# Two more PSUM banks between the native runs of medium expert pairs, and down weights loaded with two rows side by side

## The chip, the core and the metric

The kernel runs on one core of a Trainium2 chip. The metric is the device time of one execution in microseconds (us), the median of the runs. A second measure is the span of one execution under the hardware profiler, from its first to its last instruction.

The engines are TensorE (PE, with its weight loads as PEld), VectorE (DVE), ScalarE (ACT), GpSimd (POOL) and SyncE (SP, which issues nearly all DMA transfers). SBUF is the memory that the engines read, PSUM the one that TensorE writes, in eight banks of 128 partitions x 512 fp32 columns.

## What is computed

One layer of a decoder for 512 tokens of 1024 fp32 values: an attention part, a mixture of 32 experts of which each token takes four, a gated term and a last norm. The change touches only the experts:

```python
def moe(x, w_router, b_router, w_up, b_up, w_down, b_down):
    ...
    xs = xf[tok]
    h = lax.ragged_dot(xs, w_up, sizes) + b_up[sorted_e]
    g, lin = jnp.split(h, 2, axis=-1)
    g = jnp.minimum(g, SWIGLU_LIMIT)
    lin = jnp.clip(lin, -SWIGLU_LIMIT, SWIGLU_LIMIT)
    act = g * jax.nn.sigmoid(SWIGLU_ALPHA * g) * (lin + 1.0)
    y = lax.ragged_dot(act, w_down, sizes) + b_down[sorted_e]
    y = y * w.reshape(-1)[order][:, None].astype(y.dtype)
    return jax.ops.segment_sum(y, tok, num_segments=n).reshape(B, T, D)
```

Here `xf` is the normed residual, `tok` the token of each row sorted by expert, and `w` the softmax weight of each choice. Per expert `w_up` is 1024 x 2048 and `w_down` 1024 x 1024, all fp32.

## The kernel before

After attention and routing the 32 experts are sorted by how many tokens they got and given kinds: five pairs of a big (B, up to 128 tokens) and a small one (S, up to 64), then eleven pairs of a medium (M, up to 96) and a small one. Expert i is handled by `up(i)`, an activation (`act_big`, `act_medium`, `act_small`) and `down(i)`. M and S experts multiply the fp32 weights as they were loaded (a native run): the tokens stand as stationary tiles of 32 columns, and four matmuls into the four 32-row parts of a PSUM bank go side by side (`halves`). A B expert splits its weights in two rounded parts first.

**Order of a medium pair.** TensorE runs up_medium(i), down(i-1) of the small expert before, up_small(i+1), then **stretch 1**, down(i) of the medium expert, then **stretch 2**, and the next up_medium. `hooks` put other work into the two stretches, and `fence` keeps the order. Stretch 1 has these steps, each with a PSUM bank from `new_x()`:

- two times four transposes of the medium expert's activations (`rest` in `act_medium`, L1353), copied out by ACT (L1355);
- `pair_slots` of the next pair (L1043, L1046): eight small matmuls find which token stands in which slot. Eight copies on DVE bring the result to `v4` and `vx` (L1051, L1055), `fetch` turns it into indices (L993, L995), and POOL gathers the rows of the tokens with two indirect DMAs (L997);
- five times `add` (L1427): three matmuls bring the result of earlier experts back to token order, and DVE adds it to the residual `x` (L1452).

Stretch 2 has the small expert's four transposes (L1333, copied by ACT, L1334), then in turn four times four transposes of the gathered rows (`rows_T`, L1005, copied by ACT, L1011 and L1013) and the last three adds. The bias matmuls of the next run follow (L1261, L1263).

**PSUM.** Pool pU has the banks u0 to u3, pY y0 and y1, and px two banks that `new_x()` hands out in turn; a step whose bank is still read by DVE or ACT waits. up_medium writes u0, u1 and u2, up_small of such a pair u3 and u0, down(i) y0 and y1.

**Weights.** `load_next` issues one transfer of 1 MiB on SP's queue as soon as a slot is free: 128 rows of w_up (8 KB a partition), or 256 rows of w_down, of which partition p gets rows p and p + 128 (two pieces of 4 KB). A pair takes 16 transfers of w_up and 8 of w_down.

The lines of the bank and of the load:

```python
    def new_x():
        return px.tile([128, 512], F32, name="px1")
...
            src = w[:, 256 * c:256 * c + 256, :].rearrange("o (k p) f -> p (o k) f", p=128)
            t = t.rearrange("p (k f) -> p k f", k=2)
```

Of the kernel before, what the change touches and what calls it, by code (L numbers as in the profile page):

```python
# [9 lines left out]
F32 = mybir.dt.float32  # L10
# [9 lines left out]
D = 1024  # L20
# [16 lines left out]
KIND = "BS" * NB + "MS" * (16 - NB)  # L37
EO = (2 * NB - 2, 4)
CAP = {"B": 128, "M": 96, "S": 64}
KW = 5  # L40
NEW = 2
G7 = 7.0 / (1.0 + math.exp(-1.702 * 7.0))
# [16 lines left out]
def f32(ap):  # L59
    return ap.bitcast(F32)  # L60
# [3 lines left out]
def hybrid_block_kernel(  # L64
# [5 lines left out]
    nc = tc.nc  # L70
# [7 lines left out]
    identf = cp.tile([128, 128], F32, name="identf")  # L78
# [96 lines left out]
    if True:  # L175
# [27 lines left out]
        for k in range(KT):  # L203
            pt = pT.tile([128, 512], F32, name="pt")
# [22 lines left out]
        o = 0  # L227
# [493 lines left out]
    def load_next(eng=nc.sync):  # L721
        key = order[nload[0]]
        nload[0] += 1
        e, part, c = key
        t = raw_tile(key)
        raws[key] = t
        if part in ("bu", "bd"):

            src = (b_up if part == "bu" else b_down)[0].rearrange("e (b q f) -> e q b f", q=2, f=512)
            n = FF if part == "bu" else 512  # L730
            for q in range(2):
                eng.dma_start(out=t[64 * q:64 * q + NE, 0:n].rearrange("e (b f) -> e b f", f=512), in_=src[:, q])
            return
        if part in "UD" and e not in ids:

            ids[e] = nc.values_load(idi[0:1, e:e + 1], engines=[mybir.EngineType.SP], min_val=0, max_val=NE - 1)
        if part == "U":
            src = w_up[0, ds(ids[e], 1) if e else slice(0, 1), 128 * c:128 * c + 128, :].rearrange("o p f -> p (o f)")
        else:
            w = {"D": lambda: w_down[0, ds(ids[e], 1) if e else slice(0, 1)], "G": lambda: w_ple_gate,  # L740
                 "W": lambda: w_out[:, 512:]}[part]()
            src = w[:, 256 * c:256 * c + 256, :].rearrange("o (k p) f -> p (o k) f", p=128)
            t = t.rearrange("p (k f) -> p k f", k=2)
        loaded.append(eng.dma_start(out=t, in_=src))

# [28 lines left out]
    for _ in range(NRA):  # L774
        load_next()
# [20 lines left out]
    for t, key in ((bup, "bu"), (bds, "bd")):  # L796
        r = raws.pop((0, key, 0))
# [240 lines left out]
    def pair_slots(i):  # L1038

        oh = ohs[i // 2]  # L1040
        pt = new_x()
        for j in range(NT):
            nc.tensor.matmul(pt[:, 0:8], oh[:, j, 0:128], w4p[:, j, i:i + 2].rearrange("p e a -> p (e a)"),  # L1043
                             start=(j == 0), stop=(j == NT - 1))
        for j in range(NT):
            nc.tensor.matmul(pt[:, 8:12], oh[:, j, 32:160], w4p[:, j, i], start=(j == 0), stop=(j == NT - 1))  # L1046
        u, w, x = slice(0, 64), slice(64, 128), slice(96, 128)
        for e, src in ((i, pt[w, 0:4]), (i + 1, pt[u, 4:8])):
            v = v4[e] = fc.tile([C, 4], F32, name="v4", bufs=6)
            for r in (u, w):  # L1050
                nc.vector.tensor_copy(v[r], src)  # L1051

        v = vx[i] = fc.tile([C, 4], F32, name="vx", bufs=3)
        for r in range(0, 128, 32):
            nc.vector.tensor_copy(v[r:r + 32], pt[x, 8:12])  # L1055
        fetch(i)
        fetch(i + 1)
        nc.vector.tensor_tensor(v[:, 3:4], v[:, 0:1], v[:, 1:2], op=ALU.add)
        for e in (i, i + 1):
            nc.vector.tensor_tensor(wtt[:, e:e + 1], v4[e][:, 0:1], v4[e][:, 1:2], op=ALU.add)  # L1060
# [28 lines left out]
    for m in range(4):  # L1089
        mm = first_rows((3,), (m,))  # L1090
        v = pts[m].rearrange("p (k n c) -> p k n c", n=2, c=C)
# [22 lines left out]
    pU = pool(ectx, "pU", 1, space=PSUM)  # L1114
    pY = pool(ectx, "pY", 1, space=PSUM)
    px = pool(ectx, "px", 2, space=PSUM)
# [4 lines left out]
    def new_y():  # L1121
        return [pY.tile([128, 512], F32, name=f"y{s}") for s in range(2)]

    def new_x():
        return px.tile([128, 512], F32, name="px1")

    def sort_ids():
        pt = new_x()
# [49 lines left out]
    def note():  # L1178
        stretch.append(next(x for x in reversed(nc.cur_bb.bb.instructions) if x.engine == mybir.EngineType.PE))

    @contextmanager
    def fence():

        with ExitStack() as after:
            for x in stretch:
                after.enter_context(tc.issue_after(x))
            stretch.clear()
            yield

    def hooks(between, at, ins):  # L1190
        note()
        for k, f in between:
            if k == at:
                with tc.issue_after(ins):
                    f()
                note()
# [99 lines left out]

    aT = {}

    def swiglu(g, ln, pg, pl):
        nc.scalar.activation(g, pg, AF.Gelu_apprx_sigmoid)  # L1300
        nc.vector.tensor_scalar(ln, pl, 8.0, -6.0, op0=ALU.min, op1=ALU.max)  # L1301
        nc.vector.scalar_tensor_tensor(ln, g, G7, ln, op0=ALU.min, op1=ALU.mult)

    def act_big(i, ps):

        t = aT[i] = ex1.tile([128, 2, KT, C], F32R, name="ab")

        def half(b):
            ln = ex1.tile([C, 512], F32, name="aln", bufs=2)
            swiglu(ex1.tile([C, 512], F32, name="ag"), ln, ps[b], ps[2 + b])  # L1310

            def rest():
                pt = new_x()
                for k in range(4):
                    nc.tensor.transpose(pt[:, k * 128:(k + 1) * 128], ln[:, k * 128:(k + 1) * 128], identf)
                v = pt.rearrange("p (k c) -> p k c", c=C)
                nc.scalar.copy(t[:, 0, 4 * b:4 * b + 4], v)
                nc.vector.tensor_sub(t[:, 1, 4 * b:4 * b + 4], v, f32(t[:, 0, 4 * b:4 * b + 4]))

            return rest  # L1320

        return [half(b) for b in range(2)]

    def act_small(i, ps):

        t = aT[i] = ex2.tile([128, KT, 64], F32, name="am")
        ln = ex1.tile([128, 512], F32, name="aln", bufs=2)
        swiglu(ex1.tile([128, 512], F32, name="ag"), ln, *ps)

        def rest():  # L1330
            pt = new_x()
            for k in range(4):
                nc.tensor.transpose(pt[:, k * 128:(k + 1) * 128], ln[:, k * 128:(k + 1) * 128], identf)  # L1333
            nc.scalar.copy(t.rearrange("p (h k) c -> p h k c", h=2), pt.rearrange("p (k h c) -> p h k c", h=2, c=64))  # L1334

        return [rest]

    def act_medium(i, ps):

        t = ex1.tile([128, 2, KT, C], F32, name="ab").rearrange("p a k c -> p (a k c)")  # L1340
        t = aT[i] = t[:, 0:KT * 96].rearrange("p (k c) -> p k c", c=96)
        tv = t.rearrange("p (h k) c -> p h k c", h=2)
        ln, lx = (ex1.tile([128, 512], F32, name="aln", bufs=2) for _ in range(2))
        swiglu(ex1.tile([128, 512], F32, name="ag"), ln, ps[0], ps[1])
        g, u = ex1.tile([128, 512], F32, name="ag"), slice(64, 128)
        nc.scalar.activation(g[u], ps[2][0:64], AF.Gelu_apprx_sigmoid)
        nc.vector.tensor_scalar(lx, ps[2], 8.0, -6.0, op0=ALU.min, op1=ALU.max)
        nc.vector.scalar_tensor_tensor(lx[u], g[u], G7, lx[u], op0=ALU.min, op1=ALU.mult)

        def rest(src, a, b):  # L1350
            pt = new_x()
            for k in range(4):
                nc.tensor.transpose(pt[:, k * 128:(k + 1) * 128], src[:, k * 128:(k + 1) * 128], identf)  # L1353
            v = pt.rearrange("p (k q) -> p k q", q=128)[:, :, 64 * (a > 0):]
            nc.scalar.copy(tv[:, :, :, a:b], v.rearrange("p k (h c) -> p h k c", h=2))  # L1355

        return [lambda: rest(ln, 0, 64), lambda: rest(lx, 64, 96)]
# [211 lines left out]
    for i in range(NE):  # L1569
# [42 lines left out]
        nexts = gathers(i // 2 + 1) if i + 1 < NE else []  # L1612
        if KIND[i - 1] == "B":
            between = [(-1, f) for f in ahead_of] + [(HA, rest[0])] + list(zip(KS, adds)) + list(zip(HG, nexts))
            with fence():
                note()
                hooks(between, -1, stretch[-1])
                down(i - 1, between, chunks)
        else:
            behind = [f for pair in zip(nexts, adds[KW:] + [None]) for f in pair if f]  # L1620
            between = [(7 if nexts else 3, rest[0])] + [(7, f) for f in (behind or adds[KW:])]
            with fence():
                note()
                hooks([(-1, f) for f in ahead_of + adds[:KW]], -1, stretch[-1])
            with fence():
                down(i - 1, between)
        if i == 2 * NB - 1:

            slots += [[hiA[0], f"{name}{n}", -1] for name in ("hi", "lo") for n in (1, 2)]
            slots += [[mixp, "m8", -1] for _ in range(2)]  # L1630
# [152 lines left out]
```

## Time and profile before

| What | Value |
|---|---|
| runs of the kernel | 1575.9, 1576.07, 1583.03 us; median 1576.07 us |
| the profiled execution | 1576.53 us, its span 1574.9 us |
| PE (matmul) | 1484.1 us busy, 94% of the span |
| PEld (weight loads, beside PE) | 828.3 us, 53% |
| DVE | 717.1 us, 46% |
| ACT | 518.6 us, 33% |
| POOL | 313.0 us, 20% |
| mean granted TensorE clock | 0.979 of full speed |
| DMA | 452.90 MB, mean 288 GB/s; 111648 packets on SP's queue, 71.8% of 16 engines' span |

Times of rows are from the span's start. "Idle before" is how long the engine stood before an instruction, with what ended it. A busy PE is not PE at its peak: the ends of its pipelined matmuls are modelled, so two rows can overlap, and steps between starts say more. The granted clock 1.00 is 2.4 GHz, 0.50 is 1.2 GHz. The DMA share is of all 16 DMA engines and can read a little over 1.

### The profile page before, as it was taken

To read this page: it belongs to the slowest core of one execution; us is meant where nothing else is said; L and a number is where in the kernel's file an instruction comes from. 1 tells how busy PE (TensorE), PEld (TensorE's weight loads), DVE (VectorE), ACT (ScalarE), POOL (GpSimd) and SP (SyncE) were. 2 spreads that over 40 slices of the span, in tenths; PEclk is the share of its full clock that TensorE was granted. 3 is DMA by queue.
4 is the path that set the end of the run, shared out by engine and by line. 5 is a ranking of instruction groups with operands and counts; after the bars stand their busy time and mean duration, and the time that the engine had idled before them with its cause. 6 is when DMAs were issued, how large, how long until landed. Compare 5 with 4: busy or idle time off the path is not lost.

```text
span 1574.9 us, 26212 instructions
## 1 busy us (share of the span) xinstructions
PE 1484.1 (94%) x10421; PEld 828.3 (53%) x10421; DVE 717.1 (46%) x1470; ACT 518.6 (33%) x992; POOL 313.0 (20%) x469
## 2 busy tenths in 40 slices
PE   6999999999889999899899999999999999999997
PEld 5777777788554747565243333434333343433366
DVE  6578788777554856564122122212212221221165
ACT  5556666645443535342011101101110111111154
POOL 5222221122420311303021111203111130301011
PEclk9999999998999999999999999999999999999999
DMA  6240210563599999986999999999999999999611
GB/s 164 59 114 15 75 41 28 171 230 122 214 405 356 383 368 358 400 330 245 417 392 417 396 394 415 390 417 380 416 371 390 378 364 402 357 391 376 243 67 54
DMA packets 116767, 452.90 MB, mean 288 GB/s; under 512 B 11160, under 2 KB 43456, under 8 KB 83872
## 3 DMA queue, kind: packets, MB, share of 16 engines
q1 hardware_dynamic: 111648, 437.51, 71.8%
q0 software_dynamic: 3632, 10.49, 2.3%
q10 hardware_dynamic: 1360, 3.17, 0.5%
q8 instruction: 83, 1.36, 0.4%
q14 instruction: 44, 0.36, 0.1%
HBM read 444.78 MB, written 6.36 MB: 286 GB/s over the span
## 4 chain that ended last, share of the span: by engine, by line
PE 47%; DMA 4%; DVE 3%; ACT 2%; issue 1%; POOL 0%; POOLq 0%; ACTq 0%; DVEq 0%; SPq 0%
PE u L1244 18%; PE y L1244 10%; PE px L1427 5%; PE u L1273 4%; PE y L1390 2%; PE u L1715 2%; DMA raw<-in_w_down_dram 1%; DMA m<-in_w_up_dram 1%; DVE x L1452 1%; PE u L1234 1%; DMA raw<-in_w_up_dram 1%; DMA lo<-in_w_up_dram 1%; PE y L1381 0%; ACT ag L1300 0%; PE px L1333 0%
## 5 line engine op out<-in xcount | busy, mean ns | idle before, releaser
L1301 DVE TENSOR_SCALAR aln<-u 128x512 f32<-128x512 f32 x37 | 25.6, 691 | 380.9 <-PE u L1244 196.1
L1452 DVE TENSOR_TENSOR x<-x,px 128x512 f32<-128x512 f32 x120 | 81.6, 686 | 185.0 <-PE px L1427 184.1
L1300 ACT ACTIVATE ag<-u 128x512 f32<-128x512 f32 x37 | 22.2, 599 | 397.2 <-PE u L1244 176.3
L1244 PE MATMUL u<-raw,xs 128*32 128x512 f32 x976 | 111.2, 596 | 10.4 <-DMA raw<-in_w_up_dram 10.4
L1427 PE MATMUL px<-yb,so 128*128 128x512 f32 x240 | 92.9, 472 | 20.2 <-DVE vx L1055 9.1
L1080 POOL TENSOR_SCALAR so<-tok,v 128x512 fp32r<-128x512 f32 x32 | 52.7, 1648 | 226.1 <-PE px L1427 223.7
L1253 POOL TENSOR_SCALAR bsel<-blk,selp 128x128 fp32r<-128x128 f32 x11 | 6.6, 603 | 432.6 <-PE u L1292 432.6
L1234 PE MATMUL u<-hi,xb 128*128 128x512 f32 x240 | 80.0, 403 | 0.0
L1244 PEld LDWEIGHTS u<-raw,xs 128*32 128x32 f32 x976 | 30.7, 110 | 86.0 <-issue 66.0
L1334 ACT COPY am<-px 128x512 f32<-128x512 f32 x16 | 9.4, 587 | 200.8 <-PE px L1333 200.8
L763 DVE TENSOR_TENSOR lo<-raw,hi 128x1024 fp32r<-128x1024 f32 x50 | 59.3, 1221 | 28.3 <-ACT hi L762 28.3
L1427 PEld LDWEIGHTS px<-yb,so 128*128 128x128 f32 x240 | 43.9, 212 | 48.6 <-DVE x L1452 25.0
L159 PE MATMUL ps<-uh,wlo 128*128 128x512 f32 x160 | 65.3, 408 | 0.0
L762 ACT CAST hi<-raw 128x1024 fp32r<-128x1024 f32 x50 | 50.4, 1048 | 42.9 <-DMA raw<-in_w_down_dram 15.8
L159 PE MATMUL ps<-uh,whi 128*128 128x512 f32 x160 | 64.4, 403 | 0.1
L159 PE MATMUL ps<-ul,whi 128*128 128x512 f32 x160 | 64.2, 401 | 0.0
L1244 PE MATMUL u<-raw,xb 128*32 128x512 f32 x528 | 62.8, 593 | 0.0
L1409 DVE SCALAR_TENSOR_TENSOR ym<-y,wtt,ym 64x512 fp32r<-64x512 f32 x30 | 22.5, 750 | 85.1 <-ACT ym L1408 85.1
L307 ACT ACTIVATE P<-s,nm 128x256 f32<-128x256 f32 (+3 forms) x96 | 50.8, 532 | 21.5 <-DVE nm L306 20.6
L1244 PE MATMUL u<-xn,xs 128*32 128x512 f32 x448 | 52.6, 609 | 5.3 <-ACT hi L762 3.0
L150 POOL TENSOR_TENSOR wlo<-wraw,whi 128x512 fp32r<-128x512 f32 x20 | 31.8, 1594 | 104.8 <-ACT whi L148 79.9
L1427 PE MATMUL px<-ym,so 128*128 128x512 f32 x120 | 52.5, 437 | 0.0
(523 smaller groups left out, 3333.8 us busy)
## 6 DMA issues: line engine op xcount, KB each, us to landing
raw<-in_w_up_dram SPq DMA_DIRECT2D x120, 1024.0 KB, 13.4
raw<-in_w_down_dram SPq DMA_DIRECT2D x61, 1024.0 KB, 11.6
xn<-in_w_up_dram SPq DMA_DIRECT2D x55, 1024.0 KB, 11.7
xn<-in_w_down_dram SPq DMA_DIRECT2D x34, 1024.0 KB, 7.8
hi<-in_w_up_dram SPq DMA_DIRECT2D x28, 1024.0 KB, 14.7
lo<-in_w_up_dram SPq DMA_DIRECT2D x24, 1024.0 KB, 12.0
m<-in_w_up_dram SPq DMA_DIRECT2D x23, 1024.0 KB, 12.4
m<-in_w_down_dram SPq DMA_DIRECT2D x13, 1024.0 KB, 14.6
```

The lines of the kernel that those rows point to most:

```text
L150: nc.gpsimd.tensor_tensor(lo[:, 4:8], raw[:, 4:8], f32(hi[:, 4:8]), op=ALU.subtract)
L159: nc.tensor.matmul(ps, wa[:, k, :], ub[:, k, :], start=(n == 0), stop=(n == 3 * KT - 1))
L307: nc.scalar.activation(P[:, o:o + n], s[:, o:o + n], AF.Exp, bias=nm[:, u:u + 1], accum_out=sm[:, u:u + 1])
L762: split_act.append(nc.scalar.copy(hi[:, w], r[:, w]))
L763: nc.vector.tensor_tensor(lo[:, w], r[:, w], f32(hi[:, w]), op=ALU.subtract)
L1080: nc.gpsimd.tensor_scalar(so[i], tok, v4[i][:, 2:3], None, op0=ALU.is_equal)
L1234: mm = nc.tensor.matmul(ps[s], a, b[:, w], start=(i + k + n == 0), stop=(k == KT - 1 and n == 2))
L1244: mm = nc.tensor.matmul(ps[r:r + 32], x[:, c:c + 32], w, start=start, stop=stop)
L1273: nc.tensor.matmul(ps[2][32 * s:32 * s + 32], x[:, k, 64:96], raw[:, 512 * s:512 * s + 512], start=False, stop=stop)
L1390: mm = nc.tensor.matmul(ps[1][r:r + 32], t[:, 2 * c + m, 64:96], raw[:, o:o + 512], start=(c == 0), stop=(c == 3))
L1427: nc.tensor.matmul(ps, so[o][:, 128 * t:128 * t + 128], y, start=(first and not m), stop=(m == len(terms) - 1))
L1452: nc.vector.tensor_tensor(xs[t][:, w], xs[t][:, w], pt, op=ALU.add)
```

## The change

`new_x()` takes names from a list first: in stretch 1 the eight banks are px, u1, px, u2, px, u1, px, u2, in stretch 2 the first four are u1, px, u2, px and the rest px. The four copies into `v4` go from DVE to ACT. A transfer of w_down gives partition p the neighbouring rows 2p and 2p + 1, one piece of 8 KB, and so the transposes of all activations take every second column (`every`).

```diff
+SP1 = (None, "u1", None, "u2") * 2
+SP2 = ("u1", None, "u2", None)
...
-            src = w[:, 256 * c:256 * c + 256, :].rearrange("o (k p) f -> p (o k) f", p=128)
+
+            src = w[:, 256 * c:256 * c + 256, :].rearrange(
+                "o (p k) f -> p (o k) f" if part == "D" else "o (k p) f -> p (o k) f", p=128)
...
             for r in (u, w):
-                nc.vector.tensor_copy(v[r], src)
+                nc.scalar.copy(v[r], src)
...
+    spare = []
+
     def new_x():
-        return px.tile([128, 512], F32, name="px1")
+        name = spare.pop(0) if spare else None
+        return pU.tile([128, 512], F32, name=name) if name else px.tile([128, 512], F32, name="px1")
...
+    def every(a, k):
+
+        return a[:, 256 * (k // 2):256 * (k // 2) + 256].rearrange("p (c k) -> p k c", k=2)[:, k % 2]
...
-                nc.tensor.transpose(pt[:, k * 128:(k + 1) * 128], src[:, k * 128:(k + 1) * 128], identf)
+                nc.tensor.transpose(pt[:, k * 128:(k + 1) * 128], every(src, k), identf)
...
             with fence():
                 note()
+                spare.extend(SP1)
                 hooks([(-1, f) for f in ahead_of + adds[:KW]], -1, stretch[-1])
+                spare.clear()
             with fence():
+                spare.extend(SP2 if nexts else ())
                 down(i - 1, between)
+                spare.clear()
```

The same line of `transpose` changes in `act_big` and `act_small`. Three places show what moves. The first is PE in stretch 1 of a medium pair, from its transposes (lines stand 4 to 11 further down in the changed kernel; `px1` is a px bank, `u1` and `u2` are banks of pU, the number behind is the use; `aln` holds activations, `w4p` and `sqa` the slots, `yb` and `ym` results of medium and small experts, `so` where they belong). Before:

```order
L1353 MATMUL px1_8132<-identf_60,aln_7960 128x128 [waits DVE_49]
L1353 MATMUL px1_8132<-identf_60,aln_7960 128x128 x3
L1353 MATMUL px1_8138<-identf_60,aln_7961 128x128 [waits DVE_49]
L1353 MATMUL px1_8138<-identf_60,aln_7961 128x128 x3
L1043 MATMUL px1_8144<-w4p_4307,sqa_7970 128x8 [waits Activation_49]
L1043 MATMUL px1_8144<-w4p_4307,sqa_7970 128x8 x3
L1046 MATMUL px1_8144<-w4p_4307,sqa_7970 128x4 x4
L1427 MATMUL px1_8174<-yb_7814,so_7979 128x512 [waits Activation_49]
L1427 MATMUL px1_8174<-yb_7814,so_7981 128x512
L1427 MATMUL px1_8174<-ym_8026,so_7983 128x512 [waits DVE_49]
L1427 MATMUL px1_8179<-yb_7814,so_7979 128x512 [waits DVE_49,PE_49]
L1427 MATMUL px1_8179<-yb_7814,so_7981 128x512
```

Now:

```order
L1364 MATMUL px1_8132<-identf_60,aln_7960 128x128 [waits DVE_49]
L1364 MATMUL px1_8132<-identf_60,aln_7960 128x128 x3
L1364 MATMUL u1_8138<-identf_60,aln_7961 128x128 [waits DVE_49,PE_49]
L1364 MATMUL u1_8138<-identf_60,aln_7961 128x128 x3
L1047 MATMUL px1_8144<-w4p_4307,sqa_7970 128x8 x4
L1050 MATMUL px1_8144<-w4p_4307,sqa_7970 128x4 x4
L1438 MATMUL u2_8174<-yb_7814,so_7979 128x512 [waits Activation_49]
L1438 MATMUL u2_8174<-yb_7814,so_7981 128x512
L1438 MATMUL u2_8174<-ym_8026,so_7983 128x512 [waits DVE_49]
L1438 MATMUL px1_8179<-yb_7814,so_7979 128x512 [waits Activation_49]
L1438 MATMUL px1_8179<-yb_7814,so_7981 128x512
L1438 MATMUL px1_8179<-ym_8026,so_7983 128x512 [waits DVE_49]
```

The second transposes and the first add stand in u1 and u2, the slots no longer wait for ACT, and the second add starts behind a wait for ACT where it waited for DVE.

The second place is PE in stretch 2 (`xn` are the gathered rows). Before:

```order
L1333 MATMUL px1_8257<-identf_60,aln_8125 128x128 [waits DVE_49]
L1333 MATMUL px1_8257<-identf_60,aln_8125 128x128 x3
L1005 MATMUL px1_8263<-identf_60,xn_4652 128x128 [waits DMASW0_49,DVE_49]
L1005 MATMUL px1_8263<-identf_60,xn_4652 128x128 x3
L1427 MATMUL px1_8269<-yb_7814,so_7979 128x512 [waits Activation_49]
L1427 MATMUL px1_8269<-yb_7814,so_7981 128x512
L1427 MATMUL px1_8269<-ym_8026,so_7983 128x512
L1005 MATMUL px1_8274<-identf_60,xn_4652 128x128 [waits Activation_49]
L1005 MATMUL px1_8274<-identf_60,xn_4652 128x128 x3
L1427 MATMUL px1_8280<-yb_7814,so_7979 128x512 [waits DVE_49]
L1427 MATMUL px1_8280<-yb_7814,so_7981 128x512
L1427 MATMUL px1_8280<-ym_8026,so_7983 128x512
```

Now:

```order
L1344 MATMUL u1_8257<-identf_60,aln_8125 128x128 [waits DVE_49]
L1344 MATMUL u1_8257<-identf_60,aln_8125 128x128 x3
L1009 MATMUL px1_8263<-identf_60,xn_4652 128x128 [waits DMASW0_49]
L1009 MATMUL px1_8263<-identf_60,xn_4652 128x128 x3
L1438 MATMUL u2_8269<-yb_7814,so_7979 128x512 [waits DVE_49]
L1438 MATMUL u2_8269<-yb_7814,so_7981 128x512
L1438 MATMUL u2_8269<-ym_8026,so_7983 128x512
L1009 MATMUL px1_8274<-identf_60,xn_4652 128x128 x4
L1438 MATMUL px1_8280<-yb_7814,so_7979 128x512 [waits Activation_49]
L1438 MATMUL px1_8280<-yb_7814,so_7981 128x512
L1438 MATMUL px1_8280<-ym_8026,so_7983 128x512
L1009 MATMUL px1_8285<-identf_60,xn_4652 128x128 [waits DMASW7_49,Activation_49]
```

The small expert's transposes stand in u1 and the first add in u2; that add and the second transposes of gathered rows have lost their waits for ACT, and the second add waits for ACT where it waited for DVE.

The third is DVE behind the slot matmuls, in the same stretch 1 (`x8` is the residual). Before:

```order
L1051 COPY v4_8153<-px1_8144 64x4 [waits PE_49,Pool_49]
L1051 COPY v4_8153<-px1_8144 64x4
L1051 COPY v4_8156<-px1_8144 64x4 [waits Pool_49]
L1051 COPY v4_8156<-px1_8144 64x4
L1055 COPY vx_8159<-px1_8144 32x4 x4
L993 CAST ix_8164<-v4_8153 128x1 [waits DMASW5_49,DVE_49]
L993 CAST ix_8168<-v4_8156 128x1 [waits DMASW6_49,DVE_49]
L1058 TENSOR_TENSOR vx_8159<-vx_8159 128x1 [waits DVE_49]
L995 CAST ix_8164<-vx_8159 32x1 [waits DVE_49]
L1060 TENSOR_TENSOR wtt_3913<-v4_8153 128x1
L1060 TENSOR_TENSOR wtt_3913<-v4_8156 128x1
L1452 TENSOR_TENSOR x8_3443<-x8_3443,px1_8174 128x512 [waits PE_49]
```

Now, on DVE:

```order
L1059 COPY vx_8159<-px1_8144 32x4 [waits PE_49,Activation_49]
L1059 COPY vx_8159<-px1_8144 32x4 x3
L997 CAST ix_8164<-v4_8153 128x1 [waits DMASW5_49]
L997 CAST ix_8168<-v4_8156 128x1 [waits DMASW6_49]
L1062 TENSOR_TENSOR vx_8159<-vx_8159 128x1 [waits DVE_49]
L999 CAST ix_8164<-vx_8159 32x1 [waits DVE_49]
L1064 TENSOR_TENSOR wtt_3913<-v4_8153 128x1
L1064 TENSOR_TENSOR wtt_3913<-v4_8156 128x1
L1463 TENSOR_TENSOR x8_3443<-x8_3443,u2_8174 128x512 [waits PE_49]
```

and on ACT, from the copy of the medium expert's activations:

```order
L1366 COPY ab_7959<-px1_8132 128x8x64 [waits PE_49]
L1366 COPY ab_7959<-u1_8138 128x8x32 [waits PE_49]
L1055 COPY v4_8153<-px1_8144 64x4 [waits PE_49,Pool_49]
L1055 COPY v4_8153<-px1_8144 64x4
L1055 COPY v4_8156<-px1_8144 64x4 [waits Pool_49]
L1055 COPY v4_8156<-px1_8144 64x4
```

The four copies into `v4` stand on ACT behind its two copies of activations, and the copies into `vx` on DVE wait for ACT.

## Rows read from the trace of the kernel before

**Rows 1.** Windows: us, busy of each engine (instructions), TensorE clock, DMA share, GB/s.

```profile
844.50:1049.20 204.70, 197.54 (x1638) 76.11 (x1634) 47.79 (x102) 26.06 (x48) 39.08 (x60) 0.97 1.02 403
...
1117.40:1185.60 68.20, 66.11 (x550) 25.39 (x546) 15.96 (x34) 8.69 (x16) 13.02 (x20) 0.97 0.98 386
```

**Rows 2.** Windows: stretch 1 and stretch 2 of one pair.

```profile
1131.80:1141.20 9.40, 8.23 (x41) 5.58 (x38) 6.05 (x20) 1.46 (x3) 6.16 (x11) 0.82 1.00 416
1151.50:1158.70 7.20, 6.28 (x40) 4.46 (x36) 2.62 (x4) 3.33 (x7) 1.67 (x2) 1.00 1.03 422
```

**Rows 3.** Waits of PE, 776 to 1460 us: total us, times, longest us.

```profile
PE px L1427 <- DVE vx L1055: 9.1, 10, 1.2
...
PE px L1427 <- DVE x L1452: 8.5, 26, 0.4
...
PE u L1244 <- DMA lo<-in_w_up_dram: 1.1, 2, 0.6
```

**Rows 4.** Timeline of stretch 1: start us, us, engine, line, what [idle before].

```profile
1132.42 1.03 PE L1353 MATMUL px<-identf,aln 128*128 128x128 f32 x8
...
1133.69 0.61 PE L1043 MATMUL px<-w4p,sqa 128*128 128x8 f32 x4 [0.24 <-ACT ab L1355]
...
1134.61 0.71 PE L1427 MATMUL px<-yb,so 128*128 128x512 f32 x2
...
1134.85 0.70 DVE L1051 COPY v<-px 64x4 f32<-64x4 f32 x4 [0.30 <-PE px L1046]
...
1135.58 0.70 DVE L1055 COPY vx<-px 32x4 f32<-32x4 f32 x4
...
1136.43 0.93 PE L1427 MATMUL px<-yb,so 128*128 128x512 f32 x2 [0.89 <-DVE vx L1055]
...
1137.09 1.42 DVE L1452 TENSOR_TENSOR x<-x,px 128x512 f32<-128x512 f32 x2
...
1141.17 1.92 PE L1244 MATMUL y<-m,ab 128*32 128x512 f32 x16
```

**Rows 5.** Windows: two slices of 2 us in stretch 1.

```profile
1135.70:1137.70 2.00, 1.27 (x3) 0.62 (x3) 1.84 (x11) 0.00 (x0) 2.00 (x6) 0.76 1.02 426
1137.70:1139.70 2.00, 1.96 (x5) 1.49 (x5) 0.94 (x3) 0.00 (x0) 1.77 (x3) 0.50 1.00 414
```

**Rows 6.** Timeline of stretch 2, PE.

```profile
1151.61 0.66 PE L1333 MATMUL px<-identf,aln 128*128 128x128 f32 x4
...
1152.10 0.60 PE L1005 MATMUL px<-identf,xn 128*128 128x128 f32 x4
...
1152.94 0.73 PE L1427 MATMUL px<-yb,so 128*128 128x512 f32 x2 [0.24 <-ACT am L1334]
...
1154.68 0.73 PE L1427 MATMUL px<-yb,so 128*128 128x512 f32 x2 [0.34 <-DVE x L1452]
...
1157.23 0.60 PE L1005 MATMUL px<-identf,xn 128*128 128x128 f32 x4
```

**Rows 7.** Timeline, PE: additions without a wait, in a pair with a big expert.

```profile
652.93 0.62 PE L1427 MATMUL px<-yb,so 128*128 128x512 f32 x2
...
653.62 0.62 PE L1427 MATMUL px<-yb,so 128*128 128x512 f32 x2
```

**Rows 8.** Groups by line, ACT: small copies out of PSUM (mean ns after the total).

```profile
L479 ACT CAST VC<-pt 31x64 fp32r<-31x64 f32 x4 | 0.6, 198 | 0.2 <-DVE VC L480 0.2
```

**Rows 9.** Timeline, PE: matmuls with a strided moving operand.

```profile
75.29 3.81 PE L442 MATMUL pt<-KX,m 128*128 128x62 f32 x32
```

**Rows 10.** Windows: 7.2 us with 4 KB packets alone, and with 8 KB packets alone.

```profile
853.20:860.40 7.20, 6.96 (x63) 2.76 (x56) 0.69 (x1) 1.36 (x3) 0.60 (x1) 1.00 1.03 410
896.40:903.60 7.20, 7.20 (x72) 2.19 (x68) 0.00 (x0) 0.00 (x0) 0.00 (x0) 1.00 1.02 423
```

**Rows 11.** The second gather of a pair, and landing times of the stage's gathers (L997).

```profile
1139.93 0.93 POOL L997 DMA_INDIRECT xn<-xnd,ix  x1 [0.31 <-issue]
...
DMA to landing us min/median/max: 6.9/8.4/11.5
```

More of the change, by code (lines that the diff above doesn't have):

```diff
@@ L1314, in rest @@
                 for k in range(4):
-                    nc.tensor.transpose(pt[:, k * 128:(k + 1) * 128], ln[:, k * 128:(k + 1) * 128], identf)
+                    nc.tensor.transpose(pt[:, k * 128:(k + 1) * 128], every(ln, k), identf)
                 v = pt.rearrange("p (k c) -> p k c", c=C)
@@ L1332, in rest @@
             for k in range(4):
-                nc.tensor.transpose(pt[:, k * 128:(k + 1) * 128], ln[:, k * 128:(k + 1) * 128], identf)
+                nc.tensor.transpose(pt[:, k * 128:(k + 1) * 128], every(ln, k), identf)
             nc.scalar.copy(t.rearrange("p (h k) c -> p h k c", h=2), pt.rearrange("p (k h c) -> p h k c", h=2, c=64))
```

## The prediction

> **What bounds the kernel now.** I read four views in this order: the stretches of the long stage with medium pairs, the list of waits of TensorE, the timeline of one pair, and the DMA rows. From about 790 us to 1460 us the program repeats one pair every 68.2 us. In [rows 1] PE is busy 66.1 of 68.2 us, and the DMA engines are busy all the time, so two things are near their limit at once. First TensorE: the reader should see in [rows 2] that two pieces of a pair run differently. Stretch 1 (between the up run of the small expert and the down run of the medium one) takes 9.4 us at a granted clock of 0.82, and stretch 2 (between that down run and the next up run) 7.2 us at 1.00. In [rows 3] PE's longest waits of the stage sit in these two stretches: for the DVE copies into vx and for the DVE additions into x. They are waits for one of the two px banks. Second DMA: the weights that a pair consumes are 24 transfers of 1 MiB, 25.17 MB, and the two gathers of at most 160 rows of 4 KB add 0.66 MB, with instructions about 25.9 MB. While the queue is never empty it moves 403 GB/s [rows 1], so one pair cannot be shorter than 25.9 / 0.403 = 64.3 us. TensorE is the bound by 4 us, and DMA is next.
>
> **Stretch 1, part by part.** [Rows 4] show it in one pair. PE starts the eight transposes at 1132.42 and the eight small slot matmuls at 1133.69, 0.24 us late, for a px bank that ACT still reads. It adds once at 1134.61. The second add starts at 1136.43 after 0.89 us without work, because its bank holds the slots, which DVE copies out in eight copies (0.70 and 0.70 us). Then the clock falls: in [rows 5] it is 0.76 in one slice and 0.50, the lower level of 1.2 GHz, in the next, after a stretch of transposes, slot matmuls and that hole. The remaining adds run at half rate, and the down run starts at 1141.17.
>
> After the change the eight uses of a bank go px, u1, px, u2, px, u1, px, u2. I walk them with the same durations. Four transposes take 0.49 us ([rows 6], 1151.61 to 1152.10), so the slots start at 1132.42 + 0.98 = 1133.40, 0.29 earlier, and the first add (u2) at 1134.32. An add without a wait takes 0.69 us [rows 7]: the second starts at 1135.01 (px; its ACT copy ended long before), the third at 1135.70 (u1), the fourth at 1136.39 if the slots are out of px. Here the moved copies count. Four copies of 64x4 now stand on ACT, and by the order of the program DVE's four vx copies wait for them. Nothing else is queued on ACT there. The trace has no such copy on ACT; the nearest are ACT copies of 31x64 at 198 ns [rows 8] and DVE's own four in 0.70 us [rows 4], so I take 0.75 us (bounds 0.70 and 0.8). They start 0.29 earlier than DVE's did, at 1134.56, end at 1135.31, and vx runs from about 1135.45 to 1136.15. The fourth add does not wait. What is late next is DVE: from the start of vx to the first addition it needs 1137.09 - 1135.58 = 1.51 us, so that addition runs from 1136.96 to 1137.67 (two take 1.42). The fifth add needs that bank (u2). PE is free at 1137.08, starts at 1137.7 and ends at 1138.4; the down run starts at 1138.5 instead of 1141.17. **Gain 2.7 us** if the clock stays up. DVE's later additions fall into the down run, where nobody waits for them before stretch 2.
>
> **Stretch 2.** [Rows 6]: now three adds each wait (0.24, 0.34 and, like the second, 0.34 us), and the step from add to add is 1.74 us where 0.69 + 0.49 would do. After the change rest takes u1, the first add u2, the others px. With 0.49 per four transposes, starts are 1151.61, 1152.10, the add at 1152.6, transposes at 1153.3, the second add at 1153.75. The third transposes wait about 0.1 us for ACT, and the third add for DVE as before, 1.74 us behind the second: 1155.5. The last transposes come at 1156.2 instead of 1157.23. **Gain 1.0 us.** The next up run writes u1 and u2 again; their readers ended 2 us before.
>
> **Strided transposes.** The down rows now lie in pairs, so the transposes of the activations load every second fp32 column. No row shows a strided weight load. The nearest is a matmul with a strided moving operand (KX, a step of 16 columns): 32 in 3.81 us, 0.119 each for 62 columns [rows 9], the step of an ordinary transpose. If that step were all the strided read, 128 columns would need 0.245, 0.125 more; twelve transposes a pair would cost 1.5 us. Bounds 0 and 1.5 us a pair; I take 0, since the row shows no slower step. The Trainium skill (SBUF — State Buffer, Door 1: The DMA port swizzle) says that fp32 reads keep full bandwidth while two accesses fall into one 16-byte line; by it the price is 0 too, and no run here shows it.
>
> **Down weights.** Packets double from 4 to 8 KB, as the up weights have. [Rows 10]: a slice with down packets alone moves 410 GB/s, one with up packets alone 423. A pair's 8.39 MB of down weights then take 0.6 us less, and the DMA limit of a pair goes from 64.3 to 63.7 us. A transfer of 1 MiB lands 0.08 us sooner. Where PE waits for a transfer today ([rows 3], the first medium pair) that is the gain, a few tenths at most; I book 0. SP issues as many transfers as before.
>
> **Sum.** Ten pairs have both stretches (ten waits for vx in [rows 3]): 10 x (2.7 + 1.0) = 37 us. The new pair is 64.5 us, above the DMA limit of 63.7, so the loads stay hidden, with little to spare. The gathers do too: the second is issued at 1139.93 today, 0.29 earlier then, and lands at most 11.5 us later [rows 11], at 1151.1; its rows are transposed third in stretch 2, at 1154.5 - 2.7 = 1151.8. The profiled execution took 1576.53 us (span 1574.9), 0.5 above the median of the runs: 1576.5 - 37 = 1539.5, so **1539 us**. What a measurement of this kernel can tell from no change is about 0.5%, 8 us.
>
> **Rivals.** *The clock falls all the same.* Transposes and slot matmuls still fill 1.9 us of stretch 1. If 1.2 GHz is granted from 1136.7 to past 1139.7 as now (half of the slice at 0.76 and all of the slice at 0.50 [rows 5]), the end of the fourth add, the fifth and the first matmuls of the down run take double: 0.3 + 0.7 + 0.3 = 1.3 us given back in each of ten pairs, a gain of 24, 1552. Against it: in stretch 2 adds and transposes alternate with holes and the clock is 1.00 throughout [rows 2]. The Trainium skill (TensorE: Matmul & The Clock Gate, Part 4: PE-mode transpose) says that transposes do not count as busy as matmuls do; by it this rival would decide, and stretch 2 as it is speaks neither way. Chance 0.12.
>
> *DMA becomes the bound.* The lead of the loads at the first pair is none, PE waits for single chunks there [rows 3]. If longer packets bring nothing and jitter of the gathers drops the rate to 395 GB/s, a pair takes 25.9 / 0.395 = 65.6 us: gain 26, 1550. Against it: 403 holds the gathers already. It decides once PE's pair is under DMA's. Chance 0.10.
>
> *Slower.* A strided weight load at a third of the rate would add 0.3 us to each transpose; the program has 192 of the activations (12 for each of 16 pairs), 58 us against 37, 1597. It decides from 0.235 us each, twice the bound of [rows 9]. Chance 0.03. *A strided load of 0.125:* 192 x 0.125 = 24 given back, 1563, chance 0.05. That the banks aren't used is excluded by the order.
>
> **Numbers.** Forecast 0.70, its own range 1529 (DMA limit 63.7: ten pairs of 4.5) to 1546; with the rivals 1527 to 1558. Faster by over 0.5% 0.95, within 0.5% 0.02, slower 0.03.
>
> **What would show it.** Right: the pair at 64 to 65 us, stretch 1 near 6.7 and stretch 2 near 6.2 us, clock 1.00 in both, one PE wait of some 0.6 us for x in stretch 1, none for vx, four transposes still in 0.49 us, half as many down packets. Wrong: clock 0.50 in stretch 1; waits of u or y for weights in every pair; wider steps between transposes.

## The result and the profile after

The changed kernel takes 1551.99 us (median of 4 runs, 1551.46 to 1553.7) against 1579.55 us of the kernel before beside it: a ratio of 0.9839, with a 95% interval of 0.9811 to 0.9866. So it is faster by 1.6%, well above the 0.5% that the prediction named. It lies inside the wide range of 1527 to 1558, but outside the forecast's own range of 1529 to 1546: 13 us of the gain that was forecast are missing. The profiled execution took 1552.14 us with a span of 1550.5, 24.4 under the 1574.9 of before; the forecast was 37.

The windows of the changed kernel come first: eight pairs of the long stage (the second to the ninth), one of them, and its two stretches. Columns are those of [rows 1].

```profile
854.46:1383.27 528.81, 513.72 (x4372) 199.15 (x4368) 119.98 (x240) 75.18 (x160) 104.51 (x160) 1.00 1.01 405
...
1119.44:1125.93 6.49, 6.23 (x37) 4.88 (x33) 4.39 (x15) 2.08 (x7) 4.36 (x10) 1.00 1.01 422
1136.37:1144.18 7.81, 6.03 (x37) 4.44 (x33) 2.60 (x4) 3.41 (x7) 1.60 (x2) 1.00 1.01 405
1119.44:1185.52 66.08, 64.05 (x550) 24.72 (x546) 14.98 (x30) 9.40 (x20) 13.06 (x20) 1.00 1.01 406
```

A pair takes 528.81 / 8 = 66.10 us where it took 68.2 [rows 1]. Stretch 1, from the biases of the small expert to the down run, is 6.49 us at a granted clock of 1.00; measured between the same two instructions it was 9.32 (1131.85 to 1141.17 [rows 4]). Stretch 2 was to shrink to about 6.1 and has grown instead: 7.81 from its first transposes to the next up run, against 7.07 (1151.61 to 1158.68). The two ends that the rows of before do not show:

```profile
1131.85 0.73 PE L1292 MATMUL u<-bup,bsel 128*128 128x512 f32 x2
...
1158.68 1.92 PE L1244 MATMUL u<-xn,xb 128*32 128x512 f32 x16
```

The first three rows of the list of waits of PE, 770 to 1460 us (total us, times, longest), tell why:

```profile
PE px L1009 <- DMA xn<-xnd,ix: 10.7, 8, 1.8
PE u L1438 <- DVE x L1463: 2.8, 10, 0.3
PE px L1438 <- DVE x L1463: 2.6, 10, 0.3
```

The waits for vx [rows 3] are gone, and those for x have fallen from 8.5 to 5.4 us. In their place stands one that the list of before does not have: the transposes of gathered rows (L1009) wait for the gather. The two stretches of one pair in the timeline of PE, with the rows of ACT, DVE and POOL that they hang on:

```profile
1120.01 0.63 PE L1364 MATMUL px<-identf,aln 128*128 128x128 f32 x4
1120.48 0.64 PE L1364 MATMUL u<-identf,aln 128*128 128x128 f32 x4
1120.88 0.59 PE L1047 MATMUL px<-w4p,sqa 128*128 128x8 f32 x4
...
1121.77 0.70 PE L1438 MATMUL u<-yb,so 128*128 128x512 f32 x2
...
1125.04 0.73 PE L1438 MATMUL u<-yb,so 128*128 128x512 f32 x2 [0.26 <-DVE x L1463]
...
1136.37 0.74 PE L1344 MATMUL u<-identf,aln 128*128 128x128 f32 x4
1138.63 0.66 PE L1009 MATMUL px<-identf,xn 128*128 128x128 f32 x4 [1.52 <-DMA xn<-xnd,ix]
...
1122.00 0.67 ACT L1055 COPY v<-px 64x4 f32<-64x4 f32 x4 [0.46 <-PE px L1050]
...
1122.76 0.70 DVE L1059 COPY vx<-px 32x4 f32<-32x4 f32 x4 [0.59 <-PE u L1438]
...
1124.29 0.69 DVE L1463 TENSOR_TENSOR x<-x,u 128x512 f32<-128x512 f32 x1
...
1125.87 0.96 POOL L1001 DMA_INDIRECT xn<-xnd,ix  x1 [0.16 <-issue]
1127.14 0.93 POOL L1001 DMA_INDIRECT xn<-xnd,ix  x1 [0.30 <-DVE x L1463]
```

Stretch 1 is the walk of the prediction almost row for row. Stretch 2 stops behind `rest` for 1.52 us: PE comes to the gathered rows at 1136.9, and they land at about 1138.6, 11.5 us after the second gather's issue. Which gather that is shows in the order of the built program on POOL, from the down run's start on:

```order
392 L1001 DMA xn<-xnd,ix 64x1024
393 L1001 DMA xn<-xnd,ix 96x1024
```

The 64 rows of the small expert are fetched first and the 96 of the medium one second, while `rows_T` transposes the medium rows first, directly behind `rest`. The source alone does not show it: there `pair_slots` calls `fetch` for the medium expert first, but the medium expert's indices need one more instruction on DVE (L999, from `vx`), and the built order has its gather second.

### The profile page after: what moved, and what is told of

It reads as the page before. It is cut to its first block, busy times and chain, and to the rows that moved or that the text cites. A ratio compares the mean times of both kernels' runs of the same rounds, so it can differ in the third digit from the quotient of the medians.

```text
span 1550.5 us, 26223 instructions
## 1 busy us (share of the span) xinstructions
PE 1465.5 (95%) x10421; PEld 822.9 (53%) x10421; DVE 708.3 (46%) x1426; ACT 526.0 (34%) x1036; POOL 313.7 (20%) x469
## 4 chain that ended last, share of the span: by engine, by line
PE 42%; DMA 8%; POOL 3%; DVE 2%; issue 1%; ACT 0%; POOLq 0%; ACTq 0%
PE u L1251 20%; PE y L1251 7%; DMA xn<-xnd,ix 6%; PE u L1280 5%; PE u L1730 2%; PE px L1438 2%; DMA m<-in_w_up_dram 1%; PE px L1009 1%; POOL sqa L881 1%; POOL sqa L880 1%; PE u L1241 1%; PE u L1438 1%; DMA raw<-in_w_up_dram 1%; PE y L1401 1%; PE y L1392 1%
## 5 line engine op out<-in xcount | busy, mean ns | idle before, releaser
L1463 DVE TENSOR_TENSOR x<-x,u 128x512 f32<-128x512 f32 x42 | 28.7, 683 | 125.2 <-PE u L1438 124.9
L1463 DVE TENSOR_TENSOR x<-x,px 128x512 f32<-128x512 f32 x78 | 53.3, 684 | 42.0 <-PE px L1438 41.9
L161 PE MATMUL ps<-ul,whi 128*128 128x512 f32 x160 | 64.5, 403 | 0.0
L1438 PE MATMUL px<-yb,so 128*128 128x512 f32 x156 | 52.4, 417 | 2.9 <-DVE x L1463 2.9
L1345 ACT COPY am<-u 128x512 f32<-128x512 f32 x10 | 5.9, 585 | 144.8 <-PE u L1344 144.8
L1009 PE MATMUL px<-identf,xn 128*128 128x128 f32 x240 | 38.2, 283 | 17.3 <-DMA xn<-xnd,ix 17.3
```

Source lines behind the costliest of these rows:

```text
L161: nc.tensor.matmul(ps, wa[:, k, :], ub[:, k, :], start=(n == 0), stop=(n == 3 * KT - 1))
L1009: nc.tensor.transpose(pt[:, 128 * k:128 * k + 128], r[:, 512 * h + 128 * k:512 * h + 128 * k + 128], identf)
L1438: nc.tensor.matmul(ps, so[o][:, 128 * t:128 * t + 128], y, start=(first and not m), stop=(m == len(terms) - 1))
L1463: nc.vector.tensor_tensor(xs[t][:, w], xs[t][:, w], pt, op=ALU.add)
```

## The experiments

All runs stand beside the kernel before on their own chip. The medium stage begins at anything from 786 to 799 us in the profiles (more on this at the end), which moves a whole run by several us; so beside the ratio each row has the pair: eight pairs in the profile, second to ninth, divided by eight.

| Kernel | median us | ratio to before (95%) | pair, us | GB/s | PE waits for gathered rows, us |
|---|---|---|---|---|---|
| before | | 1 | 68.28 | 391 | none |
| the change | 1551.99 | 0.9839 (0.9811 to 0.9866) | 66.10 | 405 | 10.7 |
| layout alone | 1577.33 | 0.9983 (0.9953 to 1.0013) | 68.23 | 391 | none |
| banks alone | 1550.33 | 0.98 (0.9759 to 0.9841) | 66.16 | 402 | 8.5 |
| copies on DVE | 1554.7 | 0.982 (0.9775 to 0.9865) | 66.17 | 404 | 6.8 |
| small rows first | 1536.31 | 0.9718 (0.967 to 0.9766) | 64.39 | 405 | none |
| small rows first, again | 1540.14 | 0.9732 (0.9696 to 0.9769) | 64.33 | 406 | none |
| ... stretch 1's banks alone | 1555.29 | 0.9844 (0.9799 to 0.9889) | 65.44 | 406 | none |
| ... copies on DVE | 1548.32 | 0.9804 (0.9773 to 0.9835) | 65.08 | 406 | none |
| ... 4 KB packets | 1546.31 | 0.9797 (0.976 to 0.9833) | 64.77 | 402 | none |
| ... four banks | 1538.14 | 0.9747 (0.9708 to 0.9786) | 64.34 | 406 | 0.7 |
| ... four banks, 4 KB packets | 1541.86 | 0.9784 (0.9746 to 0.9821) | 64.88 | 402 | 1.0 |
| one add in u1 | 1565.05 | 0.992 (0.9894 to 0.9946) | 67.08 | 399 | 1.6 |

### The parts of the change, one by one

**Layout alone.** The new layout and its transposes; no bank and no copy moves.

```diff
-                nc.scalar.copy(v[r], src)
+                nc.vector.tensor_copy(v[r], src)
...
-                spare.extend(SP1)
...
-                spare.extend(SP2 if nexts else ())
```

> Kernel before with only the new layout of the down weights and the strided transposes that go with it. Theory (the gain comes from the banks; strided loads are free; longer packets only raise the DMA limit, which does not bind a pair of 68.2 us): 1574 to 1577 us on the scale where the kernel before takes 1576. Rival (longer packets carry part of the gain): 1568 or less. Rival (strided loads cost): above 1580.

No difference that can be told: 0.9983, pairs of 68.23. The waits are those of before (9.2 us for vx, 8.3 for x). A side finding in three of its pairs, here one at 1061 us, in the timeline of PE:

```profile
1061.01 0.74 PE L1299 MATMUL u<-bup,bsel 128*128 128x512 f32 x2
...
1065.63 0.70 PE L1438 MATMUL px<-yb,so 128*128 128x512 f32 x2 [0.89 <-DVE vx L1059]
...
1069.68 1.92 PE L1251 MATMUL y<-raw,ab 128*32 128x512 f32 x16
```

The hole of 0.89 us is there, and yet the adds behind it run at full rate (0.70 for two, 0.93 in [rows 4]); the window 1065.7 to 1069.7 has a granted clock of 1.00. From the biases to the down run this stretch 1 takes 8.67 us against 9.32: the fall of the clock cost about 0.65 us a pair there, the waits the rest of the 2.83. Within this one run the pairs say nearly the same, 67.61 us without the fall and 68.30 with it.

**Banks alone.** The extra banks with the old layout, and the copies on DVE.

```diff
-                nc.scalar.copy(v[r], src)
+                nc.vector.tensor_copy(v[r], src)
...
-                "o (p k) f -> p (o k) f" if part == "D" else "o (k p) f -> p (o k) f", p=128)
+                "o (k p) f -> p (o k) f", p=128)
...
-        return a[:, 256 * (k // 2):256 * (k // 2) + 256].rearrange("p (c k) -> p k c", k=2)[:, k % 2]
+        return a[:, k * 128:(k + 1) * 128]
```

> Only the two banks in turn: old layout of the down weights, v4 copies on DVE. Theory (the second gather is what stretch 2 now waits for, and it does not depend on the layout): 1550 to 1556 us, a wait for the gather of 1 to 2 us in nine pairs. Rival (DMA as a whole is now the bound of a pair, so packets of 4 KB cost 0.6 us in each of ten pairs and PE waits for weights): 1558 to 1562.

66.16 us a pair, as the whole change. The two banks carry nearly all of its gain. One of the change's eight pairs lost its clock (67.95 us, see the clock rival below); the other seven average 65.84, the same seven here 66.04 and in the next run 66.12. So behind the wait for the gather the copies and the layout together add some 0.2 us a pair.

**Copies on DVE.** The change, with the `v4` copies back on DVE (first two lines of the diff above).

> The changed kernel with the four v4 copies back on DVE. Theory (ACT's 0.67 us and the hand-over take as long as DVE's own 0.70 us, and the fifth add waits for DVE either way): within 2 us of the changed kernel's 1552. Rival (the copies on ACT free DVE and carry part of the gain): 1555 or more.

66.17 against 66.10. The median, 1554.7, lies between the theory's bound and the rival's, and decides nothing. But the waits show that this is a sum of two: PE now waits 2.4 us for vx and 5.2 (before 2.8) for x in u, and 6.8 instead of 10.7 us for the gather. What comes late in stretch 1 is taken from the wait behind it.

### The gather

**Small rows first.** The changed kernel, with the gathered rows transposed in the order of their issue.

```diff
-        return [lambda kind=kind, h=h: rows_T(q, kind, h) for kind in KIND[2 * q:2 * q + 2] for h in range(2)]
+        kinds = KIND[2 * q:2 * q + 2]
+        return [lambda kind=kind, h=h: rows_T(q, kind, h) for kind in (kinds[::-1] if kinds == "MS" else kinds)
+                for h in range(2)]
```

> The changed kernel, but in medium pairs stretch 2 transposes the rows of the small expert (gathered first, 64 rows) before those of the medium one (gathered second, 96 rows). Theory (PE waits at the first transposes only because they read the gather that was issued second): the wait for the gather goes, some 1.7 us in nine pairs, 1552 - 15 = 1537 us. Rival (DMA is the bound and the wait turns up elsewhere, at the weights or the third transposes): 1547 to 1552.

The wait is gone and the pair is 64.39 us. Its windows, eight pairs and one stretch 2, and the row that now follows `rest`:

```profile
854.28:1369.38 515.10, 509.99 (x4372) 197.49 (x4368) 119.99 (x240) 74.41 (x160) 104.53 (x160) 1.00 1.01 405
...
1129.03:1135.08 6.05, 5.71 (x38) 4.43 (x34) 2.60 (x4) 3.20 (x7) 1.58 (x2) 1.00 1.00 405
```

```profile
1129.61 0.60 PE L1009 MATMUL px<-identf,xn 128*128 128x128 f32 x4
```

Stretch 2 takes 6.05 us, 1.76 less than in the changed kernel. With a median of 1536.3 us it is the best kernel of the study beside the one with four banks, and faster than both kernels of the case. A second series on another chip agrees in the pair, 64.33:

> The changed kernel with the small expert's rows transposed first, once more, beside the next two on the same chip. Both theories: a pair of 64.4 us and about 1536 us.

### What each part is worth once the gather is out of the way

**Stretch 1's banks alone.** As small rows first, without the list for stretch 2 (`SP2`).

```diff
-                spare.extend(SP2 if nexts else ())
```

> The run with the small expert's rows transposed first (1536.3 us), but with the two extra banks in stretch 1 alone. Theory: the gather now hides, TensorE sets the pair of 64.3 us, and the banks of stretch 2 are worth 1.0 us in each of ten pairs: a pair of 65.3 us, 1546 us. Rival: the DMA engines set the pair by now (about 25.9 MB at 403 GB/s are 64.3 us), so that the 1.0 us lies beside them: 1537 us. In between would mean that the longer stretch 2 hides part of something else, and its PE waits should tell what.

A pair of 65.44, 1.05 us more than 64.39 (1.11 more than in the second series): the banks of stretch 2 are worth what the theory said. The median of 1555.29 is 9 us above the expectation; in its profile the stage begins at 795.95 us, 6 later than with small rows first, for which nothing in the edit accounts; together with ten pairs of some 1.1 us this makes up the 16.6 us between the two spans (1552.1 and 1535.5).

**Copies on DVE, small rows first.**

> The same with the four v4 copies back on DVE. Theory: in the run with the old row order a stretch 1 with these copies on DVE takes 0.5 us more (0.20 us for vx, and 0.54 in place of 0.26 for x), and the wait for the gather that followed took it back (6.8 us in place of 10.7); without that wait it shows: a pair of 64.8 to 64.9 us, 1541 us. Rival: the moved copies are worth nothing by themselves (0.14 us a pair as in the run with the old row order): 64.5 us, 1537 us.

A pair of 65.08, 0.72 more than the mean of the two series with the copies on ACT. The theory holds, and its price was too low. The timeline shows the difference between a wait and a step:

```profile
1117.94 0.61 PE L1440 MATMUL u<-yb,so 128*128 128x512 f32 x2
...
1119.00 0.70 PE L1440 MATMUL px<-yb,so 128*128 128x512 f32 x2 [0.21 <-DVE vx L1061]
...
1120.47 0.73 PE L1440 MATMUL u<-yb,so 128*128 128x512 f32 x2 [0.55 <-DVE x L1465]
```

An add without a wait follows after 0.69 [rows 7]. The one with a named wait of 0.21 comes 1.06 later, so the wait costs 0.37; the next, with 0.55, comes 1.47 later and costs 0.78.

**4 KB packets, small rows first.** Old layout and neighbouring columns (the last four lines of the diff of banks alone).

> The same with the down weights in packets of 4 KB and the transposes of neighbouring columns, the copies on ACT. Theory: TensorE's pair of 64.3 us is now at the DMA limit, which four banks with 4 KB packets showed as 64.9 us: a pair of 64.8 us with waits for weights, 1540 us. Rival: the layout matters only below TensorE's pair: 64.4 us and no more waits for weights than with 8 KB, 1536 us.

A pair of 64.77, 0.4 more: its pairs lie between 64.20 and 65.41 us, with waits for weights of up to 0.61 us, while with 8 KB packets eight of the first nine lie between 64.31 and 64.35. The medians on this chip, 1546.31 against 1540.14, lie the same way and both above what was expected. The 8 KB packets do nothing for the change as it was made (banks alone and copies on DVE differ in the layout alone: 66.16 and 66.17), and about 0.4 us a pair once TensorE's pair is at the limit of the DMA.

**Four banks, with 8 KB and with 4 KB packets.** Small rows first, and u3 and u0 in turn too.

```diff
-SP1 = (None, "u1", None, "u2") * 2
-SP2 = ("u1", None, "u2", None)
+SP1 = (None, "u1", None, "u2", None, "u1", "u3", "u0")
+SP2 = ("u1", None, "u2", None, "u1", None, "u3")
```

> The same run with four banks of pU in turn in both stretches (u1, u2, u3, u0 and px), so that no add and no transposition waits for the reader of the use two before it. Theory: the fifth add's wait of 0.3 us and stretch 2's waits of 0.5 us go, PE's pair would be 63.5 us, and the DMA limit of 63.7 to 64.3 us ends the gain: 1530 to 1536 us, with waits for weights (u, y or a chunk of the loads) or for gathered rows where there were none. Rival: no DMA limit yet, 1528 us and no such waits. Second rival: the uses of u3 and u0 wait for the run that wrote them, and nothing is gained: 1536 us with waits of px uses for ACT or DVE in their place.

> The run with four banks, but with the down weights in packets of 4 KB and the transposes of neighbouring columns, as in the kernel before. Theory: once DMA sets the pair, packets of 4 KB (410 against 423 GB/s in the kernel before) cost up to 0.6 us a pair: 3 to 6 us more than with 8 KB. Rival: DMA does not set the pair, and both layouts take the same within 2 us.

The waits of PE, 785 to 1440 us, with 8 KB:

```profile
PE u L1253 <- DMA xn<-in_w_up_dram: 2.5, 5, 0.6
PE u L1253 <- DMA lo<-in_w_up_dram: 1.9, 3, 0.8
PE u L1253 <- DMA raw<-in_w_up_dram: 1.8, 4, 0.6
PE u L1253 <- DMA m<-in_w_up_dram: 1.1, 2, 0.6
PE px L1009 <- DMA xn<-xnd,ix: 0.7, 2, 0.4
PE u L1253 <- DMA hi<-in_w_up_dram: 0.6, 1, 0.6
```

No use of a bank waits any longer, and every wait left is for the DMA. The eight pairs, with 8 KB and then with 4 KB:

```profile
858.17:1372.86 514.69, 508.46 (x4372) 196.69 (x4368) 120.08 (x240) 74.53 (x160) 104.85 (x160) 1.00 1.01 406
```

```profile
853.82:1372.85 519.03, 508.92 (x4373) 194.24 (x4369) 120.33 (x240) 74.41 (x160) 104.86 (x160) 1.00 1.02 402
```

64.34 and 64.88 us: nothing under small rows first, and 0.54 between the packet sizes. The DMA sets the pair, as the theory has it; the first median is 2 us above the range that it gave. The medians (1538.14 and 1541.86) lie the same way as the pairs, though their intervals overlap.

### The hole and the clock

**One add in u1.** The kernel before, with the second add alone in another bank.

```diff
-        return px.tile([128, 512], F32, name="px1")
+        name = spare.pop(0) if spare else None
+        return pU.tile([128, 512], F32, name=name) if name else px.tile([128, 512], F32, name="px1")
...
+SP1 = (None, None, None, None, "u1")
...
+                spare.extend(SP1)
```

> The kernel before, with one use alone moved: the second add of stretch 1 goes to u1 instead of the px bank that holds the slots; stretch 2, the copies and the layout are as before. Theory of the hole: the 0.89 us without work ahead of the second add go, the third add then waits for the slots' bank or its neighbour with a shorter hole (0.2 to 0.5 us), the clock stays at 1.00 as in the changed kernel, and stretch 1 shrinks by 1.5 to 2.0 us in each of ten pairs: 1560 us. Rival: the clock falls after the transposes and slots anyway, or the hole only moves one add on: less than 0.7 us in a pair, 1573 us or more, with a granted clock of 0.5 in stretch 1.

The pair is 67.08, 1.2 us shorter; neither theory gave that. The timeline of PE, with the biases and the down run:

```profile
1134.31 0.73 PE L1299 MATMUL u<-bup,bsel 128*128 128x512 f32 x2
...
1135.67 0.48 PE L1438 MATMUL u<-yb,so 128*128 128x512 f32 x1
...
1138.88 0.70 PE L1438 MATMUL px<-yb,so 128*128 128x512 f32 x2 [0.42 <-DVE vx L1059]
...
1140.30 0.72 PE L1438 MATMUL px<-yb,so 128*128 128x512 f32 x2 [0.49 <-DVE x L1463]
...
1141.50 0.73 PE L1438 MATMUL px<-yb,so 128*128 128x512 f32 x2 [0.23 <-DVE x L1463]
1142.39 1.92 PE L1251 MATMUL y<-m,ab 128*32 128x512 f32 x16
```

Stretch 1 is 8.08 us. The clock stays at 1.00 in all ten pairs, as the theory said; but in place of the hole of 0.89 stand waits of 0.42, 0.49 and 0.23. One bank moves the wait; stretch 1 is shorter by what the clock cost, 0.65 us, and another 0.6. The run is no clean test of the hole, though. With a free bank the built order puts one matmul of the second add between the transposes and the slot matmuls (1135.67), another behind these, so what stands ahead of the adds has changed too.

## Why the prediction was right, and where it failed

The direction and stretch 1 were right by the mechanism. That 1552 us lies within the wide range is luck: its upper part was there for rivals that did not decide (1552 is the very number of the clock rival), and the loss came from a wait that the prediction had excluded.

**Stretch 1: right.** 2.7 us forecast, 2.83 measured. The copies on ACT took 0.67 us for four (0.75 taken), vx ran behind them, and the fifth add waited for DVE alone, as walked. What the prediction did not separate is that about 0.65 of it is the clock.

**Stretch 2: the size right, the end wrong.** Without the gather it takes 6.05 us against the 7.07 of before (1151.61 to 1158.68, the stretch of [rows 2]): 1.02 where 1.0 was forecast, and taking `SP2` away costs 1.05.

**The step that failed** is the sentence on the gathers in the sum: "its rows are transposed third in stretch 2, at 1154.5 - 2.7 = 1151.8". The second gather brings the medium expert's rows, and those are transposed first, behind `rest`. With the prediction's own times that is 1151.61 - 2.7 + 0.49 = 1149.4, against a landing at up to 1139.64 + 11.5 = 1151.1: 1.7 us late. The landing itself was taken rightly (11.5 us from issue in the pair shown [rows 11]). In the kernel before the same rows were needed at 1152.10 [rows 6], and this gather (L997, 1139.93) landed 9.6 us after its issue:

```profile
DMA to landing us min/median/max: 9.6/9.6/9.6
```

That is a margin of 2.5 us here and of 0.75 to 4.6 us over the ten pairs, none of which showed as a wait. Two things used it up. PE now comes to the rows 9.7 us after the issue (1127.14 to 1136.86) in place of 12.2 (1139.93 to 1152.10). And the second gather lands later: the median of ten is 11.3 us in place of 9.7, with 11.5 already in the run with the layout alone and 11.4 with the banks alone. What delays it stays open. By the landings of before, PE's earlier arrival alone would have made five of the ten pairs wait, some 6 us in all (an estimate) of the 10.7. The first pair of the changed kernel has no such wait and took 64.56 us (789.90 to 854.46), the forecast 64.5. The eight behind it took 528.81 us, against 515.10 with small rows first: 13.7 us, about what is missing. With the order that the prediction assumed (small rows first), the span is 1535.5, 39.4 under before, against 37 forecast.

**Strided transposes: nearly right.** Taken as 0 with bounds to 1.5 us a pair. Eight of them and the step to the slots take 0.87 us (1120.01 to 1120.88 above). In the run with 4 KB packets, neighbouring columns, they take 0.79:

```profile
1111.39 0.60 PE L1366 MATMUL px<-identf,aln 128*128 128x128 f32 x4
...
1112.18 0.59 PE L1049 MATMUL px<-w4p,sqa 128*128 128x8 f32 x4
```

So a strided load costs some 10 ns, 0.12 us for the twelve of a pair. The Trainium skill (SBUF — State Buffer, Door 1: The DMA port swizzle) says that reads keep full bandwidth while two accesses fall in one 16-byte line; the trace agrees but for that 0.01 us each.

**The clock rival** came true in one pair of ten, and in another place. Stretch 1 stayed at 1.00 throughout. In the pair from 1051.49 to 1119.44 (67.95 us) the clock fell behind the wait for the gather, in stretch 2, a wait that no rival had:

```profile
1070.95 0.91 PE L1009 MATMUL px<-identf,xn 128*128 128x128 f32 x4 [1.76 <-DMA xn<-xnd,ix]
1071.51 1.20 PE L1438 MATMUL u<-yb,so 128*128 128x512 f32 x2
```

The page's rule on transposes (the Trainium skill, TensorE: Matmul & The Clock Gate, Part 4: PE-mode transpose), by which this rival would have decided, did not decide here: the same transposes and slot matmuls kept 1.00 in stretch 1 of every pair.

**The DMA rival** did not decide, but it was nearer than the sum had it. The limit was put at 63.7 us with 8 KB packets and 64.3 with 4 KB; the runs that reach it show 64.3 and 64.9. The difference was right (0.54 against 0.6), the level 0.6 low: 64.34 us at 406 GB/s are 26.1 MB where 25.9 were counted at 403. At that level ten pairs give back 39 us, which puts the median's low end near 1537 and not at 1529 (ten pairs of 4.5 us from 1576.5 would have been 1531.5 in any case).

**The copies and the layout.** The prediction counted the copies only as part of the walk. With the gather hidden they are worth 0.72 us a pair; in the kernel as changed 0.07 (0.28 without the pair that lost its clock), because the wait for the gather takes up most of what they save.

## What to carry to other kernels

When a stretch is shortened, take every transfer that is issued before it and used behind it, and work out the margin of the piece that is used first, by the order of issue on its queue and the order of use in the code: a margin under the gain becomes the next wait, though the profile before shows none, and the transfer itself may take longer than before. Read the order of issue from the built program, not from the source. Parts measured one at a time behind such a wait all read as nothing; take the wait away and measure them again. Price a wait by the step between two starts, not by the idle time named beside it.

## What the runs showed of the hardware

The same hole of 0.89 us, behind the same transposes and slot matmuls, was followed by a granted clock of 0.50 in the kernel before [rows 5], and by 1.00 in three pairs of the run with the layout alone. What decides between them stays open; no run was made for it.

Profiles of one and the same kernel differ by several us before the stage begins. With small rows first the stage starts at 789.97 us in one and 796.64 in the other, while its nine pairs take 579.41 and 578.98. The windows of 300 to 420 and 420 to 480 us, first and second series:

```profile
300.00:420.00 120.00, 113.38 (x693) 98.76 (x696) 94.90 (x214) 64.93 (x114) 27.32 (x105) 0.94 0.48 179
420.00:480.00 60.00, 51.81 (x289) 32.35 (x282) 27.44 (x34) 23.02 (x28) 18.45 (x19) 0.94 1.02 408
```

```profile
300.00:420.00 120.00, 116.56 (x687) 102.06 (x687) 92.52 (x210) 62.50 (x115) 22.05 (x101) 0.90 0.43 163
420.00:480.00 60.00, 50.02 (x280) 30.47 (x279) 26.38 (x37) 23.08 (x31) 21.69 (x23) 0.89 1.00 403
```

The later one had a lower granted clock there, 0.90 and 0.89 against 0.94. That is why the parts were compared by the pair, and not by medians that lie 4 us apart for one kernel.
